# SyncE's wait for the last stores, moved behind the closing barriers of an unpooling kernel

## The chip, the cores and the metric

The kernel runs on one core of one Trainium2 chip. A core has five engines with an instruction stream each: TensorE (PE), VectorE (DVE), ScalarE (ACT), GpSimd (POOL) and SyncE (SP). [...] Transfers between HBM and the on-chip memory are issued by an engine, here SP and ACT, and carried out by 16 DMA engines; each transfer raises a semaphore by 16 when it has landed. The metric is the device time of one execution in microseconds (us), lower is better. The profile's span, from the first to the last instruction of the program, is shorter than this time: 71.0 us against 72.79 us in the execution that was profiled.

## The reference

Each input value goes to one of the four places of a 2 x 2 block of the output; the other three places are zero. Cut to what is computed:

```python
output = np.zeros((batch, channels, out_h, out_w), dtype=np.float32)
for b in range(batch):
    for c in range(channels):
        for i in range(h):
            for j in range(w):
                idx = indices[b, c, i, j]
                out_i = i * kernel_size + idx // kernel_size
                out_j = j * kernel_size + idx % kernel_size
                output[b, c, out_i, out_j] = x[b, c, i, j]
```

Here `x` is 16 x 64 x 32 x 32 in fp32, the indices run from 0 to 3, and the output is 16 x 64 x 64 x 64 in fp32. The launch hands the indices over as 64-bit integers, of which the kernel reads the lower 32-bit halves. So 4.19 MB of values and 8.39 MB of indices are read, and 16.78 MB are written.

## The kernel before

The 1024 images are spread over 128 partitions, T = 8 images to a partition. All of `x` and all indices are loaded into two tiles, `x_t` and `idx_t`, by three transfers: `x_t` (line 99, SP), the last five images' indices (line 101, SP) and the first three images' indices (line 106, ACT). Output tiles `out_t` hold G = 2 images each, so there are NG = 4 groups; three tiles are allocated, and the fourth group uses the first tile again.

VectorE makes the output. For each of the four places it runs one `scalar_tensor_tensor` (line 127): (index equals place) times x, written with strides into that place of every block. It takes two images at a time (12 instructions), and one at a time around the point where the second part of the indices begins (8 instructions). The last of each group raises `made`. Before the fourth group VectorE waits for `stored_0` (line 122), since the first store must have read the tile before it is written again.

SP stores the groups. For each it waits for `made` and issues a 4 MB transfer (line 140). The first of these raises `stored_0`, the other three raise `stored`. SP then takes `made` back to zero (line 143) and waits until `stored` has reached 48, that is, until the last three stores have landed (line 144).

The order of the work is written by hand, in two steps. First, the helper class `Program` puts the kernel's instructions into the program's first block, ahead of the branches at its end, and `first` moves the three loads ahead of the barrier with which the program opens. Second, the end of the tile context (line 175) adds a last block of its own: a drain on SP and two barriers of all engines. In a barrier the engines other than GpSimd each drain and raise one semaphore ("gather"); GpSimd waits for four of these, then raises a second semaphore ("release") by four, and each of the others waits for it and takes one off. All instructions of an engine run in the order in which they stand.

Of the kernel before, what the change touches and what calls it, by code (L numbers as in the profile page):

```python
# [1 line left out]

# [4 lines left out]

P = 128
F32 = mybir.dt.float32
I32 = mybir.dt.int32  # L10


class Program:

    def __init__(self, nc):
        self.nc = nc
        self.block = nc.main_func.blocks[0]  # L20
        self.kernel_block = nc.cur_bb.bb.name

    def __enter__(self):
        ins = self.block.instructions
        self.branches = [i for i in ins if "Branch" in type(i).__name__]
        n = len(ins) - len(self.branches)
        assert all("Branch" in type(ins[k]).__name__ for k in range(n, len(ins)))
        del ins[n:]
        self.nc.switch_bb(self.block.name, parent=None)
        self.symbolic = self.nc._always_lower_symbolic_ap  # L30
        self.nc._always_lower_symbolic_ap = False
        return self

    def first(self, made):
        ins = self.block.instructions
        assert ins[len(ins) - 1].name == made.ins.name
        moved = ins.pop()
        at = next(
            k
            for k, i in enumerate(ins)  # L40
            if i.engine == moved.engine and isinstance(i, mybir.InstDrain)
        )
        ins.insert(at, moved)

    def __exit__(self, kind, *_):
        self.nc._always_lower_symbolic_ap = self.symbolic
        if kind is None:
            for b in self.branches:
                self.block.instructions.append(b)
            self.nc.switch_bb(self.kernel_block, parent=None)  # L50


@with_exitstack
def kernel(
    ctx: ExitStack,
    tc: tile.TileContext,
    x: bass.AP,
    indices: bass.AP,
    kernel_size: bass.AP,
    out: bass.AP,  # L60
):
    nc = tc.nc
    assert kernel_size == 2

    B, C, H, W = x.shape
    n_img = B * C
    T = n_img // P
    assert T * P == n_img and C % T == 0

    G = 2  # L70
    NG = T // G
    FIRST = 3
    N = H * W
    x_v = x.rearrange("b (ch t) h w -> (b ch) (t h w)", t=T)
    idx_v = indices.rearrange("b (ch t) h w -> (b ch) (t h w)", t=T).bitcast(I32)
    out_v = out.rearrange("b (ch g t) oh ow -> g (b ch) (t oh ow)", g=NG, t=G)

    x_t = nc.alloc_sbuf_tensor("x_t", [P, T * N], F32).ap()
    idx_t = nc.alloc_sbuf_tensor("idx_t", [P, T * 2 * N], I32).ap()
    out_t = [  # L80
        nc.alloc_sbuf_tensor(f"out_t{g}", [P, G * 4 * N], F32).ap()
        for g in range(NG - 1)
    ]
    out_t.append(out_t[0])

    x_in = nc.alloc_semaphore("x_in")
    idx_in = [nc.alloc_semaphore(f"idx_in{g}") for g in range(2)]
    made = nc.alloc_semaphore("made")
    stored_0 = nc.alloc_semaphore("stored_0")
    stored = nc.alloc_semaphore("stored")  # L90

    x_c = x_t.rearrange("p (t i j) -> p t i j", t=T, j=W)
    idx_c = idx_t.rearrange("p (t i j two) -> p t i j two", t=T, j=W, two=2)[
        :, :, :, :, 0
    ]
    cut = FIRST * 2 * N

    with Program(nc) as program:
        program.first(nc.sync.dma_start(out=x_t, in_=x_v).then_inc(x_in, 16))
        program.first(  # L100
            nc.sync.dma_start(out=idx_t[:, cut:], in_=idx_v[:, cut:]).then_inc(
                idx_in[1], 16
            )
        )
        program.first(
            nc.scalar.dma_start(out=idx_t[:, :cut], in_=idx_v[:, :cut]).then_inc(
                idx_in[0], 16
            )
        )

        nc.vector.wait_ge(x_in, 16).then_inc(x_in, -16)
        for t in range(T):
            g, k = t // G, t % G
            if t in (0, FIRST):
                half = int(t == FIRST)
                nc.vector.wait_ge(idx_in[half], 16).then_inc(idx_in[half], -16)  # L116

            if k == 1 and t != FIRST:
                continue
            n = 1 if k == 1 or t + 1 == FIRST else 2  # L120
            if g == NG - 1:
                nc.vector.wait_ge(stored_0, 16).then_inc(stored_0, -16)
            o_c = out_t[g].rearrange(
                "p (m i two j wo) -> p m i two j wo", m=G, two=2, wo=2, j=W
            )
            for pidx in range(4):
                op = nc.vector.scalar_tensor_tensor(  # L127
                    out=o_c[:, k : k + n, :, pidx // 2, :, pidx % 2],
                    in0=idx_c[:, t : t + n],
                    scalar=pidx,  # L130
                    in1=x_c[:, t : t + n],
                    op0=mybir.AluOpType.is_equal,
                    op1=mybir.AluOpType.mult,
                )
            if k + n == G:
                op.then_inc(made, 1)

        for g in range(NG):
            nc.sync.wait_ge(made, g + 1)
            nc.sync.dma_start(out=out_v[g], in_=out_t[g]).then_inc(  # L140
                stored if g else stored_0, 16
            )
        nc.sync.sem_inc(made, -NG)
        nc.sync.wait_ge(stored, 16 * (NG - 1)).then_inc(stored, -16 * (NG - 1))


# [1 line left out]
_INS = ['x', 'indices', 'kernel_size']  # L148
_OUTS = [((16, 64, 64, 64), 'float32')]

_NUMBERS = {'kernel_size': 2}


# [26 lines left out]
```

## Time and profile before

| what | value |
|---|---|
| time, median of 3 runs | 72.71 us (72.57 to 72.78) |
| time of the profiled execution | 72.79 us |
| span of its profile | 71.0 us |
| VectorE busy | 35.6 us, 20 instructions, from 19.87 us on |
| stores issued (line 140) | 28.8 to 55.5 us; median 13.5 us to landing |
| SP's wait for the last stores (line 144) | 14.5 us, ends at 70.3 us |
| the rows of the closing barriers (line 175) | last start 71.0 us |

Rows named SPq, DVEq and so on are instructions that an engine's sequencer handles alone: waits, semaphore changes, drains. They are not counted as busy, and a wait's row shows the instant at which it ran, not the time that it stood waiting; that time is in the view of the waits. Rows of line 175 are those of the barriers at the end, but some of them (drains of engines that have nothing left to do) start early, the first at 1.2 us.

### The profile page before, as it was taken

To read this page: it belongs to the slowest core of one execution; us is meant where nothing else is said; L and a number is where in the kernel's file an instruction comes from. 1 tells how busy PE (TensorE), PEld (TensorE's weight loads), DVE (VectorE), ACT (ScalarE), POOL (GpSimd) and SP (SyncE) were. 2 spreads that over 40 slices of the span, in tenths; PEclk is the share of its full clock that TensorE was granted. 3 is DMA by queue.
4 is the path that set the end of the run, shared out by engine and by line. 5 is a ranking of instruction groups with operands and counts; after the bars stand their busy time and mean duration, and the time that the engine had idled before them with its cause. 6 is when DMAs were issued, how large, how long until landed. Compare 5 with 4: busy or idle time off the path is not lost.

```text
span 71.0 us, 72 instructions
## 1 busy us (share of the span) xinstructions
DVE 35.6 (50%) x20; POOL 0.2 (0%) x4
## 2 busy tenths in 40 slices
DVE  0000000000089999999999999999999200000000
POOL 1000000000000000000000000000000000000000
DMA  9598997998988999879696989899898979696980
GB/s 277 240 434 378 517 498 314 443 462 378 563 369 369 462 577 438 369 314 572 295 591 295 517 369 517 369 425 462 369 517 351 535 314 572 295 591 295 517 369 0
DMA packets 1009, 29.36 MB, mean 414 GB/s; under 512 B 113, under 2 KB 113, under 8 KB 113
## 3 DMA queue, kind: packets, MB, share of 16 engines
q1 hardware_dynamic: 864, 26.21, 86.4%
q10 hardware_dynamic: 144, 3.15, 10.3%
q14 instruction: 1, 0.00, 0.0%
HBM read 12.58 MB, written 16.78 MB: 414 GB/s over the span
## 4 chain that ended last, share of the span: by engine, by line
DVE 45%; DVEq 4%; issue 1%
DVE out_t L127 45%; DVEq L175 4%
## 5 line engine op out<-in xcount | busy, mean ns | idle before, releaser
L127 DVE SCALAR_TENSOR_TENSOR out_t<-idx_t,x_t 128x2048 f32<-128x2048 int32 (+1 forms) x20 | 35.6, 1860 | 19.9 <-DVEq L116 19.9
L161 POOL MEMSET const-bfloat16-1.0<- 128x1 bf16 x1 | 0.1, 103 | 0.0
L161 POOL MEMSET const-uint8-127<- 128x1 uint8 x1 | 0.1, 102 | 0.0
L161 POOL MEMSET const-float32-1.0<- 128x1 f32 x1 | 0.1, 100 | 0.0
L161 POOL MEMSET const-float32-0.0<- 128x1 f32 x1 | 0.1, 99 | 0.2 <-issue 0.2
## 6 DMA issues: line engine op xcount, KB each, us to landing
out_dram<-out_t SPq DMA_DIRECT2D x4, 4096.0 KB, 13.5
idx_t<-in_indices_dram SPq DMA_DIRECT2D x1, 5120.0 KB, 31.2
x_t<-in_x_dram SPq DMA_DIRECT2D x1, 4096.0 KB, 19.5
idx_t<-in_indices_dram ACTq DMA_DIRECT2D x1, 3072.0 KB, 19.6
```

What stands on the lines that cost most here:

```text
L127: op = nc.vector.scalar_tensor_tensor(out=o_c[:, k : k + n, :, pidx // 2, :, pidx % 2], in0=idx_c[:, t : t + n], scalar=pidx, in1=x_c[:, t ...
L161: nc = _bacc.Bacc("TRN2", target_bir_lowering=False, num_devices=1)
L175: with _tile.TileContext(nc) as tc:
```

## The change

SP's wait for `stored` is taken from its place in front of the last block and put at the very end of it, behind both closing barriers. A new helper, `last`, does this when the program is finalized. Each instruction is still there; on SP the order changes from "wait for the last stores, first barrier, second barrier" to "first barrier, second barrier, wait for the last stores". The aim is that the barriers need not wait for the stores, while the program still does not end before its output has landed. No other engine's instructions change.

```diff
+    def last(self, made):
+
+
+        def move(nc):
+            ins = self.block.instructions
+            at = next(k for k, i in enumerate(ins) if i.name == made.ins.name)
+            nc.main_func.blocks[-1].instructions.append(ins.pop(at))
+
+        self.nc.at_finalize(move)
...
         nc.sync.sem_inc(made, -NG)
-        nc.sync.wait_ge(stored, 16 * (NG - 1)).then_inc(stored, -16 * (NG - 1))
+        program.last(
+            nc.sync.wait_ge(stored, 16 * (NG - 1)).then_inc(stored, -16 * (NG - 1))
+        )
```

## The prediction

> **What bounds the kernel now.** I read the page first: the span, the slices, and the totals of the transfers.
>
> ```profile
> span 71.0 us, 72 instructions
> DVE  0000000000089999999999999999999200000000
> DMA  9598997998988999879696989899898979696980
> HBM read 12.58 MB, written 16.78 MB: 414 GB/s over the span
> ```
>
> The digits are tenths of busy time in fortieths of the span (1.775 us each). The DMA row is high from the first slice to the last but one; VectorE (DVE) works in the middle half only, and its last digits are zero. So the length is set by moving 29.36 MB, and the transfers leave only the last slice idle. A change that moves no transfer can gain only in that last slice and behind it. The chain of waits does not help here: it ends with VectorE's last multiply at 55.47 us, because it follows busy instructions and the stores' landing is not one.
>
> Next I cut the tail into windows. The columns after the stretch are its length, VectorE's and GpSimd's busy time, the clock, the DMA share and GB/s.
>
> ```profile
> 56.50:69.50 13.00, 0.00 (x0) 0.00 (x0) 1.00 0.96 413
> 69.50:70.00 0.50, 0.00 (x0) 0.00 (x0) 1.00 0.02 0
> 70.00:70.35 0.35, 0.00 (x0) 0.00 (x0) 1.00 0.00 0
> 70.35:71.00 0.65, 0.00 (x0) 0.00 (x0) 1.00 0.00 0
> ```
>
> The stores fill the engines until about 69.9; then nothing moves for over a microsecond. What happens there shows in the DMA queue's own waits and in the instructions of lines 144 and 175.
>
> ```profile
> SPq L144 <- SPq L144: 14.5, 1, 14.5
> L144 SPq EVENT_SEMAPHORE  x1: 17/17/17, 70.3 to 70.3; - x1
> L175 POOLq EVENT_SEMAPHORE  x4: 17/17/17, 70.5 to 70.9; - x4
> L175 SPq DRAIN  x3: 7/7/7, 70.4 to 70.7; - x3
> L175 SPq EVENT_SEMAPHORE  x2: 17/17/17, 70.6 to 70.9; - x2
> L175 DVEq EVENT_SEMAPHORE  x2: 21/21/21, 70.6 to 71.0; - x2
> L175 PEldq EVENT_SEMAPHORE  x2: 51/51/51, 70.6 to 71.0; - x2
> ```
>
> The columns behind the count are the shortest, median and longest duration in ns, then first and last start in us. SP stands 14.5 us in the wait of line 144 and leaves it at 70.3. Everything of line 175, the two closing barriers, then runs: four other engines take part, and all their release instructions start at 70.6 or later.
>
> The trace's single records give the sequence. The last store packet ends at 69.957; the last of the 48 increments of `stored` comes at 70.309; SP's wait runs at 70.326. Then SP drains at 70.404 and reports to the first barrier (drain at 70.459), GpSimd collects at 70.491 and releases at 70.570, SP passes at 70.611; SP reports again at 70.703, TensorE, the last, at 70.774, GpSimd collects at 70.819 and releases at 70.897, SP passes at 70.939, VectorE at 70.950, TensorE at 70.951. TensorE's ends at 71.002, which is the span.
>
> The measured 72.71 (72.79 in the profiled execution) is 1.7 to 1.8 us longer than the span, so something outside the program's instructions counts. The trace's records of semaphore updates continue after 71.0: semaphore 2 is raised nine times from 71.236 to 71.761 (at .236, .271, .476, .520, .543, .641, .681, .715, .761), the program's semaphores are reset one after another from 71.661 to 72.325, and semaphore 2 is raised nine times again from 72.549 to 72.906.
>
> [...] the last barrier takes 72.906 - 72.549 = 0.357 us. The barrier right behind the program takes 0.525, since its third raise comes 0.205 after the second, where the last barrier has 0.038: one engine was 0.17 late. [...] here 70.309 - 69.957 = 0.35 us. The change can't touch that.
>
> **The change part by part.** *Removed in front of the barriers:* SP's wait on `stored`. After its last store (issued at 55.496, 0.333 long) SP decrements `made` at 55.871 and goes straight to line 175. Is there another thing that would hold it there? A drain might wait for outstanding transfers. The opening barrier says no: SP's drain at 0.911 took 125 ns while the loads issued before it landed at 19.5 and 31.6. VectorE's drain ended at 55.515 and reported at 55.526, ScalarE's and TensorE's had reported at 1.295 and 1.366. So both barriers run as they do now, from SP's arrival at about 55.95 to about 56.56 (the 0.613 between SP's wait at 70.326 and its last release at 70.939). The last store hides them: it lands 14 us later. In them no engine asks the DMA engines for anything, so the store is not slowed.
>
> *Added behind the barriers:* the same wait, now SP's last instruction. Its condition is still met at 70.309, so it runs at 70.326 and ends at 70.343. Nothing of the program is queued behind it on SP, and no engine of the program waits for SP. [...]
>
> *The span:* from 71.002 to 70.343, 0.66 us less. All from the two barriers.
>
> *Behind the span:* which raise is SP's is not in the records by name; I infer the fifth[...] because the range of semaphores reset first (207 to 255, from 71.661) also runs 1.7 ns per reset, against 6 to 10 for the others, and SP has the shortest event instructions. In the kernel after, raises one to four are done long before[...]. Call this walk X, from the start of the last row to the raise. Upper bound: SP passes at 70.939 and the fifth raise is at 71.543, X at most 0.604 (it was held up behind the late third engine, so this surely counts some waiting). Nearest row: the first raise at 71.236 belongs to an engine whose last row started between 70.897 and 70.951, so 0.285 to 0.339, and this includes TensorE as the slowest sequencer (51 ns for an event where SP has 17). Lower bound: the program's entry, where the last raise is at -0.004 and the first instructions are at 0.000 to 0.131; taking the turning raise at -0.235 to SP's first instruction at 0.000 gives about 0.2. I take 0.285. The fifth raise is then at 70.326 + 0.285 = 70.611 instead of 71.543: 0.93 earlier. From there the way back, resets and final barrier are as before. Against 0.66 the extra 0.27 is the late third engine and the longer exits, hidden now because those engines arrive 14 us early. With X at 0.2 the gain is 1.02, at 0.34 0.88, at 0.604 0.61. Time: 72.71 - 0.93 = 71.78.
>
> **Rivals.** (1) *The barriers alone are gained.* If the measured time ends with the program's last instruction, or SP's walk is near its upper bound, the gain is 0.61 to 0.66: 72.05 to 72.10. For it: nothing shows where the clock of the measurement stops. Against: the time is 1.7 us longer than the span, and the resets and barriers behind it would fill most of that. (2) *No change.* If SP's walk were over 1 us, or the clock stops at something tied to the last landing alone, the new wait simply takes the barriers' place: 72.7. For it: 14.5 us of transfers still stand in front. Against: X is at most 0.604 before. (3) *Slower.* [...] The trace shows one instruction packet on queue 14, and not its cost[...]. Against: the same exit code came within 0.6 of SP's release before, and SP's wait and what follows it stand in a straight line.
>
> **How the numbers follow.** Forecast 71.78: 0.62. Rival 1, 72.05 to 72.10: 0.24. Rival 2: 0.09. Rival 3: 0.05. Runs of the kernel before spread over 72.57 to 72.78, so each case gets 0.1 either way. The forecast reaches from 1.02 gained (71.69) less that 0.1, to 71.93; rival 1 reaches to 72.2. The range 71.6 to 72.2 takes in both and leaves rivals 2 and 3 out, 0.14. Faster by over 0.3% means below 72.49: 0.62 + 0.24 = 0.86; the same 0.09; slower 0.05.
>
> **What would show it.** The span should be near 70.34, with SP's wait its last row; all rows of line 175's barriers (a later line in the changed file) near 55.9 to 56.6; DMA rows and VectorE's rows unmoved, last landing near 70.31. In the semaphore records, four raises of semaphore 2 before 58 and the fifth some 0.3 after SP's wait, then the same resets. The forecast is wrong if the barriers still wait past 70 (a drain that does hold on transfers), if the fifth raise comes 0.6 or more after SP's wait, or if the span shrinks by 0.66 and the time by no more than that.

## The result and the profile after

The changed kernel takes 71.66 us (median of 4 runs, 71.54 to 71.74) against 72.69 (72.57 to 72.78, 4 runs) for the kernel before, run beside it: a ratio of 0.9858, 95% interval 0.9835 to 0.988, so 1.03 us or 1.4% faster. The forecast was 71.78 within 71.6 to 72.2.

The page of the changed kernel, span, slices and totals as before:

```profile
span 70.4 us, 72 instructions
DVE  0000000000069999999999999999999500000000
DMA  9597996998988899969799896979797998969790
HBM read 12.58 MB, written 16.78 MB: 417 GB/s over the span
```

The same number of instructions, the same bytes, the same shape of the transfers' row; only the span is shorter. SP's own waits (engine and line, what it waited for, total us, times, longest us), and the rows of the closing barriers, now line 187, and of the wait, now line 155:

```profile
SPq L155 <- SPq L155: 13.8, 1, 13.8
SPq L187 <- PEq L187: 0.4, 2, 0.3
```

```profile
L187 POOLq EVENT_SEMAPHORE  x4: 17/17/17, 56.2 to 56.6; - x4
L187 SPq DRAIN  x3: 7/7/63, 56.0 to 56.4; - x3
L187 SPq EVENT_SEMAPHORE  x2: 17/17/17, 56.3 to 56.6; - x2
L187 PEldq EVENT_SEMAPHORE  x2: 51/51/51, 56.3 to 56.6; - x2
```

```profile
L155 SPq EVENT_SEMAPHORE  x1: 17/17/17, 70.4 to 70.4; - x1
```

The barriers' releases ran from 70.6 on before; now all are past at 56.6, under the last store, and SP's wait is the program's last row. SP's rows run in the order in which its instructions stand: line 153 at 55.946, the two barriers from 56.020 to 56.620, the wait at 70.383. In between the transfers go on as they did:

```profile
56.50:69.50 13.00, 0.00 (x0) 0.00 (x0) 1.00 0.95 408
69.50:70.05 0.55, 0.00 (x0) 0.00 (x0) 1.00 0.01 0
70.05:70.40 0.35, 0.00 (x0) 0.00 (x0) 1.00 0.00 0
```

A share of 0.95 and 408 GB/s stand against 0.96 and 413: the barriers beside the store did not slow it measurably. In this profiled execution the last packet ended at 70.013 and the last increment came at 70.367, each 0.06 later than in the profile of before. The last store was issued 0.07 later, too (55.570 against 55.496); from its issue to its landing it took 14.80 us, against 14.81 before.

What the span doesn't show is in the trace's records of semaphore updates. No instruction of the program in either trace names semaphore 2. Of its last eighteen raises the first nine are here called the exit barrier and the last nine the final barrier; the single updates of 244 semaphores (226 in the changed kernel's trace), which begin behind the fifth raise and end ahead of the final barrier, are called resets. Who makes them no record says; the recorded expectations say "the runtime's barrier" for the exit barrier. The table has the nine raises of the exit barrier in us from the span's start, with SP's wait ahead of them:

| | SP's wait | raises 1 to 4 | 5 | 6 | 7 | 8 | 9 | first and last raise of the final barrier | time of this execution |
|---|---|---|---|---|---|---|---|---|---|
| before | 70.326 | 71.236, .271, .476, .520 | 71.543 | 71.641 | 71.681 | 71.715 | 71.761 | 72.549, 72.906 | 72.79 |
| after | 70.383 | 56.919, .953, 57.158, .201 | 70.535 | 70.579 | 70.617 | 70.651 | 70.699 | 71.487, 71.845 | 71.73 |

Two readings. From raise 9 to the final barrier both take 0.788 us, and the final barrier takes 0.357 and 0.358: what follows the exit barrier took the same time in both. And the time is the last raise less 0.116 and 0.115, so the measured time goes with the last raise of the final barrier, not with the span. What the change gained is therefore the stretch from SP's wait to raise 9: 1.435 us before, 0.316 after, 1.119 less. The 1.06 between the two profiled times is this less the 0.06 by which the store landed later.

The records also show that the late wait was not overtaken in this execution: the first reset came at 70.655, behind SP's raise, and that of `stored` itself at 71.026, 0.64 after SP's wait had run (70.383).

### The profile page after: what moved, and what is told of

The parts are those of the page before. It is cut to its first block, busy times and chain, and to the rows that moved or that the text cites. A ratio compares the mean times of both kernels' runs of the same rounds, so it can differ in the third digit from the quotient of the medians.

```text
span 70.4 us, 72 instructions
## 1 busy us (share of the span) xinstructions
DVE 35.6 (51%) x20; POOL 0.2 (0%) x4
## 4 chain that ended last, share of the span: by engine, by line
DVE 46%; DVEq 4%; issue 1%
DVE out_t L137 46%; DVEq L187 4%
```

## The experiments

All times below are medians against runs of the kernel before on the same chip (72.69 to 72.74). Because the landing of the last store wanders by 0.2 us between profiles, the stretch from the last wait to raise 9 is given beside each time; it is free of that, but each is read from one profiled execution.

**e1: the wait between the two barriers.**

```diff
-            nc.main_func.blocks[-1].instructions.append(ins.pop(at))
+            end = nc.main_func.blocks[-1].instructions
+            first = next(
+                k
+                for k, i in enumerate(end)
+                if i.engine == made.ins.engine
+                and isinstance(i, mybir.InstEventSemaphore)
+            )
+            end.insert(first + 1, ins.pop(at))
```

> SP's wait stands between the two closing barriers. Theory A (the gain is what stood between the last landing and SP's arrival in the runtime's barrier: the two program barriers, 0.61, and an exit that all five engines then take at once, 0.45): the first barrier is hidden, the second is on the path, with SP as its last reporter; SP's release comes some 0.21 us after its wait instead of 0.61, and the exit behind it stays as it was before. Time 72.69 - 0.40 = 72.29. Rival B (the position matters, only a wait that is the very last instruction gains): 72.7. Rival C (any hidden barrier also hides the late exit): 71.66 + 0.21 = 71.87.

Measured: 72.35 us, ratio 0.9956 (0.994 to 0.9971); wait to raise 9: 1.048 us, 0.387 less than before. The barriers' rows in its profile (line 194; first and last start at the end):

```profile
L194 POOLq EVENT_SEMAPHORE  x4: 17/17/17, 56.0 to 70.5; - x4
L194 PEldq DRAIN  x2: 8/8/8, 1.3 to 56.3; - x2
L194 SPq EVENT_SEMAPHORE  x2: 17/17/17, 56.1 to 70.5; - x2
L194 PEldq EVENT_SEMAPHORE  x2: 51/51/51, 56.1 to 70.5; - x2
```

Of each semaphore row, half is at 56 and half at 70.5: one barrier hidden, one on the path. TensorE's second drain is at 56.3, so the others had reported long before SP came, and SP passes 0.226 us after its wait (70.502 less 70.276) where the two barriers took 0.613. Behind it the raises have the old pattern, the third 0.205 after the second. Theory A holds; B and C fall: a wait that is not last gains in part, and one hidden barrier does not hide the exit.

**e2: no closing barriers at all, the wait in its old place.**

```diff
-            at = next(k for k, i in enumerate(ins) if i.name == made.ins.name)
-            nc.main_func.blocks[-1].instructions.append(ins.pop(at))
+            del nc.main_func.blocks[-1].instructions[:]
```

> Both closing barriers are left out, with all that stood in the last block; SP's wait is back in its old place, ahead of SP's branch. Theory A (the barriers were the cost, not the place of the wait): as fast as the changed kernel but for the branch, 71.66 to 71.74. Rival B (the gain needs the wait to be the last instruction, so that what follows it is ready): clearly slower than the changed kernel, towards 72.7.

Measured: 71.67 us, ratio 0.9854 (0.9842 to 0.9867); wait to raise 9: 0.316, the changed kernel's number. The program is shorter by 23 instructions, and SP waits as long as in the kernel before:

```profile
span 70.3 us, 49 instructions
SPq L154 <- SPq L154: 14.5, 1, 14.5
```

So the place behind the barriers is worth nothing that shows in the time; the point is that no barrier stands behind the wait. Rival B falls, and with it the fear of an exit that is not ready. One difference is left: from raise 9 to the final barrier it took 0.829 us, not 0.788, and so did e9 (0.828), whose last block is empty too. The reason is open.

**e3: two more barriers behind the wait** in the kernel before.

```diff
         nc.sync.wait_ge(stored, 16 * (NG - 1)).then_inc(stored, -16 * (NG - 1))
+        nc.all_engine_barrier()
+        nc.all_engine_barrier()
```

> The kernel before with two more barriers of all engines behind SP's wait, so four in a row on the path. Theory A: each costs the 0.30 to 0.33 that one costs in the profile of before: 72.69 + 0.65 = 73.34. Rival C (most of the barriers' cost is one exit, paid once): 72.7 to 72.9.

Measured: 73.39 us, ratio 1.0095 (1.0082 to 1.0109), 0.70 more; wait to raise 9: 2.081, 0.646 more. The four barriers' releases on SP, lines 145, 146 and twice 177, run at

```profile
L145 SPq EVENT_SEMAPHORE  x1: 17/17/17, 70.5 to 70.5; - x1
```

```profile
L146 SPq EVENT_SEMAPHORE  x1: 17/17/17, 70.8 to 70.8; - x1
```

```profile
L177 SPq EVENT_SEMAPHORE  x2: 17/17/17, 71.2 to 71.5; - x2
```

(70.517, 70.845, 71.172, 71.544 in the single records): the first release comes 0.231 after the wait (70.286), and the three barriers behind it cost 0.33 to 0.37 each. The stretch from the last release to raise 9 is 0.823, against 0.822 before. Rival C falls.

**e4: the same two extra barriers, with the wait last.**

```diff
         program.last(
             nc.sync.wait_ge(stored, 16 * (NG - 1)).then_inc(stored, -16 * (NG - 1))
         )
+        nc.all_engine_barrier()
+        nc.all_engine_barrier()
```

> The changed kernel with two more barriers ahead of its closing ones, four in all, SP's wait last. Theory A: all four are hidden by the last store, 71.66. Rival D (barriers beside the store slow it or are only partly hidden): 71.8 or more.

Measured: 71.69 us, ratio 0.9859 (0.9846 to 0.9871); wait to raise 9: 0.315. Four barriers cost as much as two, that is, nothing that shows. Rival D falls. The last of them and the wait in its profile:

```profile
L189 PEldq EVENT_SEMAPHORE  x2: 51/51/51, 56.7 to 57.1; - x2
```

```profile
L155 SPq EVENT_SEMAPHORE  x1: 17/17/17, 70.3 to 70.3; - x1
```

**e5 to e8: another engine waits last.** Each changes one word of the changed kernel, here for ScalarE (then `vector`, `gpsimd`, `tensor`):

```diff
         program.last(
-            nc.sync.wait_ge(stored, 16 * (NG - 1)).then_inc(stored, -16 * (NG - 1))
+            nc.scalar.wait_ge(stored, 16 * (NG - 1)).then_inc(stored, -16 * (NG - 1))
         )
```

> As the changed kernel, but ScalarE, not SP, waits for the stores as its last instruction. Theory A: the runtime's barrier is a count that passes through the engines in a fixed order, and the time follows from the place of the late engine in it: the raises before it are done early, those behind it come after. With ScalarE second (0.32 of hops behind it) and a walk of about 0.2: 0.2 us later than the changed kernel, 71.85. Rival E (the place doesn't matter, each late engine costs the same): 71.66.

> As the changed kernel, but VectorE waits for the stores as its last instruction. Theory A: if VectorE is fourth in the barrier's order, with a walk of about 0.2, 71.75; if it is the third engine that was 0.17 late in the kernel before (walk of 0.53 to 0.58), 72.1. Rival E (the place and the engine don't matter): 71.66.

> As the changed kernel, but GpSimd waits for the stores as its last instruction. Theory A: if GpSimd is the third engine, late by 0.17 in the kernel before (walk of 0.53 to 0.58, then 0.28 of hops), 72.15; if it is fourth with a walk of about 0.2, 71.75. Rival E (the place and the engine don't matter): 71.66.

> As the changed kernel, but TensorE waits for the stores as its last instruction. Theory A: TensorE is first in the barrier's order (walk 0.285, then all eight hops, 0.36, against SP's 0.152 and 0.164): 71.66 + 0.33 = 71.99, with no raise at all before 70. Rival E (the place and the engine don't matter): 71.66.

A "raise" is one increment of semaphore 2. The raises that come before 58 us tell the place of the engine in the count: in these five profiles the raises from its own on came after its wait. "Walk" is from the start of the wait's row to that engine's raise, "hops" from there to raise 9.

| last wait on | time (ratio, interval) | raises before 58 us | walk | hops | sum |
|---|---|---|---|---|---|
| SP (changed kernel) | 71.66 (0.9858, 0.9835 to 0.988) | 4 | 0.152 | 0.164 | 0.316 |
| VectorE, e6 | 71.70 (0.9864, 0.985 to 0.9877) | 3 | 0.204 | 0.242 | 0.446 |
| ScalarE, e5 | 71.78 (0.9873, 0.9858 to 0.9888) | 1 | 0.161 | 0.324 | 0.485 |
| TensorE, e8 | 72.04 (0.9912, 0.9898 to 0.9925) | 0 | 0.326 | 0.359 | 0.685 |
| GpSimd, e7 | 72.19 (0.9933, 0.9921 to 0.9946) | 2 | 0.578 | 0.285 | 0.863 |

So the first five raises are those of TensorE, ScalarE, GpSimd, VectorE and SP, in this order. Whose the four behind SP's are, no record says; the prediction's turning raise and way back were my reading of them. Times and sums rise together, and rival E falls for TensorE and GpSimd beyond doubt; VectorE's 0.13 and ScalarE's 0.17 against SP show in the records only, as their intervals overlap the changed kernel's. In e7's profile the wait itself is as early as any other,

```profile
L155 POOLq EVENT_SEMAPHORE  x1: 17/17/17, 70.2 to 70.2; - x1
```

and its span of 70.2 us is shorter than the changed kernel's 70.4, because the last store landed 0.19 earlier in this execution. Yet this execution took 72.09 us, against 71.73: the whole loss lies behind the span.

**e9: a barrier without GpSimd behind the wait.** The last block is left out, and SP itself collects and releases:

```diff
...
+        for engine in others:
+            engine.sem_inc(here, 1)
         program.last(
             nc.sync.wait_ge(stored, 16 * (NG - 1)).then_inc(stored, -16 * (NG - 1))
         )
+        nc.sync.wait_ge(here, 3).then_inc(here, -3)
+        nc.sync.sem_inc(leave, 3)
+        for engine in others:
+            engine.wait_ge(leave, 1).then_inc(leave, -1)
...
-            at = next(k for k, i in enumerate(ins) if i.name == made.ins.name)
-            nc.main_func.blocks[-1].instructions.append(ins.pop(at))
+            del nc.main_func.blocks[-1].instructions[:]
```

(`others` are ScalarE, VectorE and TensorE; `here` and `leave` are two new semaphores, and with the last block empty the wait stays where it is written.)

> The last block with its two barriers is left out; in its place stands one barrier behind SP's wait in which SP collects and releases and only ScalarE, VectorE and TensorE take part. GpSimd is at the runtime's barrier from the start. Theory A (GpSimd's exit of 0.58 was the late third raise): the third raise now follows the second by 0.04, not 0.205; TensorE's exit (0.18 to its release, [...]0.33 of walk, 0.36 of hops) sets the end, 0.91 after SP's wait instead of the changed kernel's 0.316: 72.25. Rival F (the third raise is late whenever the engines leave together, whichever engine was held): 0.205 again between the raises, 72.42.

Measured: 72.18 us, ratio 0.9914 (0.9901 to 0.9928); wait to raise 9: 0.818, where I had expected 0.91. The raises are at 70.831, .865, .904, .948, .971 and on: the third follows the second by 0.039. With GpSimd already there, the late third raise is gone, so it was GpSimd's. Rival F falls. The three engines that leave this barrier run their last rows here:

```profile
L164 ACTq EVENT_SEMAPHORE  x1: 17/17/17, 70.5 to 70.5; - x1
L164 DVEq EVENT_SEMAPHORE  x1: 21/21/21, 70.5 to 70.5; - x1
L164 PEldq EVENT_SEMAPHORE  x1: 51/51/51, 70.5 to 70.5; - x1
```

The sum that I had expected was too long by 0.09 for two reasons. TensorE took 0.282 from its row (70.549) to its raise, not the 0.33 of e8; and the 0.91 is 0.04 more than 0.18, 0.33 and 0.36 make, an allowance that no trace shows. 0.177 to TensorE's row, 0.282 and 0.359 of hops are the 0.818.

## Why the prediction was right

**What bounds the kernel, and what hides the barriers:** right. Transfers and VectorE's work did not change. SP's drains did not wait for the stores in flight: the first, at 56.0, took 63 ns, the two behind it 7 ns each, and the store went on for 14 us. e4 shows the hiding by doubling what is hidden.

**The removed barriers, 0.61 us:** right in size. SP passed its last release 0.613 after its wait before, and e1 (one of the two left) and e3 (two more) give the price of one on the path: 0.23 with SP the only late reporter, and 0.33 to 0.37 right behind another barrier. In the kernel before the two are 0.285 (SP drains twice there) and 0.328.

**Where the measured time ends:** the forecast rested on its ending behind the final barrier, and rival 1 on its ending with the span. In all eleven profiles the time is the last raise of semaphore 2 less 0.114 to 0.125 us; rival 1 is out, e7 most plainly. Rivals 2 and 3 are out by the measured gain. Rival 3, a slower exit, rested on a cost that no trace shows; SP's whole way from its wait to its raise took 0.152 us. From the stores' last packet to the last increment of `stored` it took 0.33 to 0.36 us in all eleven profiles: the change left it where it was.

**SP's walk X:** that the fifth raise waits for SP was right (raises 1 to 4 were past at 57.201), the size was off by 0.133, and this is the larger of the two terms that leave the forecast short. I took 0.285 from the first raise and called 0.2 a lower bound; it was 0.152 (0.154 in e2, 0.151 in e4). The 0.285 was TensorE's: e8 shows that the first raise is TensorE's, and its walk was 0.281 to 0.286 in the other ten profiles. In e8 itself, with the wait on TensorE, it was 0.326; no run tests why. The slower engine's exit was the wrong row to borrow. The bound from the program's entry, from the fifth of the nine raises there (-0.235) to SP's first row (0.000), was no bound: it is the way from a raise into the program, not out of it.

**The inference that SP is fifth, and one engine late:** right; e5 to e8 show the order, e7 and e9 that the late one is GpSimd. But that SP is fifth was a guess on thin ground. SP's event instructions are not the shortest: ScalarE's and GpSimd's take 17 ns as well. And the other ranges were reset at 5 to 8 ns apiece, not 6 to 10; what is left of the argument is the 1.7 ns of the first range, and no record shows which engine resets a range. In the kernel before, GpSimd's last event is at 70.897 and the third raise at 71.476, 0.579 later, the same walk as e7's 0.578. So the late third raise was set by GpSimd's exit, which started only with its release of the second barrier.

**The way back, "as before":** wrong by 0.054. Between raise 5 and 6 there are 0.098 us before and 0.044 after. In every kernel in which VectorE had raised long before SP came, the gap is 0.043 or 0.044; where it had raised just before, 0.098 or 0.099. No run tests why.

The sum, with the measured terms: 0.613 (barriers) + 0.604 - 0.152 (from SP's release to its raise) + 0.054 (from raise 5 to 6) = 1.119, all of the change in that stretch. The forecast had 0.93, and 1.02 at the most, for it. That the time came out nearer to the forecast than this, 1.03 faster, is in part luck: in the profiled execution the later landing took back 0.06.

## What to carry to other kernels

Look at what stands behind the last landing, instruction by instruction, and move everything that does not need the stored data in front of the wait; the cost lay in the length of that chain and not in its busy time: a barrier on the path cost 0.23 to 0.37 us here, with rows of 7 to 51 ns. Put the last wait on the engine with the shortest way out that stands latest in the count, here SP (0.152 us, fifth), and let the other engines, GpSimd (0.578 us) above all, finish early; against VectorE and ScalarE this choice is worth 0.13 and 0.17 us in the records, too little to show in these times. The span can mislead on such a change: e7 has a shorter span than the changed kernel (70.2 us against 70.4) and a longer time (72.19 against 71.66).

## What the runs showed of the hardware

- The ways out differ by engine: from the start of the last wait to the engine's raise in the exit barrier SP took 0.152 us, ScalarE 0.161, VectorE 0.204, TensorE 0.326, GpSimd 0.578. ScalarE's and VectorE's numbers are from one execution each. Where TensorE left a barrier of the program instead, it took 0.281 to 0.286 in ten profiles; GpSimd took 0.578 to 0.585 in all eight in which its raise was not held up.
- From the last raise of the exit barrier to the first of the final barrier it took 0.787 to 0.789 us in nine of the eleven profiles, whichever engine had come last, and 0.829 and 0.828 in e2 and e9; engines that had come 14 us early gained nothing there.
- The first reset came 0.12 us after the fifth raise in all eleven profiles, and so after the wait for the stores, whichever engine waited.
- A drain on SP did not wait for stores in flight. In the changed kernel the first after the last store's issue took 63 ns, the next two, with the store still in flight, 7 ns each.
